# Giving out the tiles of the next moving operand up to two steps sooner in the feed-forward part of a layer, taking them at the split, and a rearranged last block

## The chip, the cores and the metric

One core of a Trainium2 chip runs the whole program. The metric is device time in microseconds (us), of one launch; lower is better. Engines are named as the profile names them: PE (TensorE matmuls), PEld (its weight loads), DVE (VectorE), ACT (ScalarE), POOL (GpSimd), SP (SyncE, which issues most of the transfers). L123 is a line of the kernel before. In the changed kernel the same statements stand 1 line further down after L1136, 10 further from the middle of `phases` on and up to 12 further in the last function.

## The reference

The kernel computes one layer of a streaming encoder on 2048 tokens of width 1024, in fp32: token mixing (sliding-window attention beside a gated recurrence), cross-attention into 256 memory tokens, and a SwiGLU feed-forward part of width 2816. Only the last part and the passage into it matter here:

```python
u = rms_norm(h, g_x_pre[l])
m = rms_norm(mem, g_mem[l])
y = cross_attention(u, m, wq_x[l], wk_x[l], wv_x[l], wo_x[l])
h = h + rms_norm(y, g_x_post[l])
u = rms_norm(h, g_ffn_pre[l])
y = (jax.nn.silu(u @ w_gate[l]) * (u @ w_up[l])) @ w_down[l]
h = h + rms_norm(y, g_ffn_post[l])
```

## The kernel before, in words

**Products.** A matrix product of fp32 accuracy is made of three matmuls of a reduced type: each operand is split into a high part (a rounded copy) and a low part (what the copy lacks), and `products` (L1270, L1271, L1272) issues high·high, high stationary·low moving, low stationary·high moving, for each of `nk` slices of 128 along the contraction. On top of that a block of 256 by 1024 outputs is made by seven products in place of eight (`seven`, a scheme of Strassen's kind). In the order of `STEPS` they are 1, 5, 6, 3, 7, 2, 4; each is `3·nk` matmuls of 128x512. Products 1, 6, 7 and 4 share one PSUM bank, 5 and 3 a second, 2 has a third, so a bank has to be emptied between them: products 1, 5 and 6 by a copy to a `part` tile (L1285 on ACT; L1287 on DVE where the last two blocks add something), the others by the block's own `out`.

**Jobs and blocks.** `phases` runs a list of jobs: 0 to 2 (attention output, scores, values; 8 blocks each), 3 and 4 (the feed-forward part's first product, one job per half of the tokens, 22 blocks each, gate and up in turn), 5, 6 and 7 (the down projection in three pieces of the contraction, nk = 3, 4, 4, 8 blocks of two row tiles each). Within a job the seven moving tiles `T` (one per product) stay in place over all blocks; the stationary tiles `S` are made anew for each block (`streamed`; ACT copies, DVE subtracts).

**Moving tiles.** There are seven slots for `T`, four in the pool `big` and three in `tb`. `uses` holds for each moving tile the steps that use it; a step `g` is one product. After each step, `half(g, ...)` looks whether the slot that comes free first is free by now (`free[1] > g`); if so it takes the next tile of the queue, allocates it, and starts the loads of its first half (the first slices of the contraction) into one or two `row` tiles (a pool of 12); at the next call its second half. It puts the half's split into `pending`, due at step `g + lag(k)`, where `lag` is 2 for tiles that are loaded ready-made. `split(g)` runs one due entry: it copies the half into the high part on ACT (L1106) and subtracts on DVE into the low part (L1109). In the last block of a job and the first of the next, a second `split(g)` a step, and after three of the steps a second `half`, are run. If a tile is needed whose halves aren't split, `Ready.__getitem__` forces them.

**What sets the order.** Each engine executes its instructions in one fixed order, which the tile scheduler derives from the program: it follows the written order as a priority and lets ready instructions pass others. `behind()` pins the splits behind the last ACT and DVE instructions written before them.

**Around the passage into job 3.** The value blocks of job 2 end with a chain (`value_block.after`): normalise (L1765), add (L1769), squares on ACT, factor on POOL, L1778 on DVE, transposes on PE and copies on ACT (L1532), stores to `u_d`, from which the moving tiles of jobs 3 and 4 are loaded. The hidden blocks evacuate with L1807 (DVE add), L1809 (Silu on ACT, with a table load when ACT's function set changes), L1816 and L1818.

**The last block.** `down_block.out` adds (L1856 or L1858), squares on ACT (L1641), multiplies by the gain in place (L1865, which must wait for the square's reading), then p_v and p_r on POOL (L1868, L1871), the final multiply-add on DVE (L1874) and a store by SP.

Of the kernel before, what the change touches and what calls it, by code (L numbers as in the profile page):

```python
# [12 lines left out]
F32R = mybir.dt.float32r  # L13
I32 = mybir.dt.int32
AF = mybir.ActivationFunctionType
ALU = mybir.AluOpType
AX = mybir.AxisListType

P = 128
T = 2048  # L20
# [10 lines left out]
EPS = 1e-6  # L31
# [17 lines left out]
class Layer:  # L49
# [1063 lines left out]
    def resident(self, get, nk, key, dst, keep, sums):  # L1113

        nc = self.nc
        halves = [(0, (nk + 1) // 2), ((nk + 1) // 2, nk)]

        def fetched(a, b):  # L1120
            if key in self.BLOCK:
                return get(*self.BLOCK[key], a, b - a), None
            if sums:
                return get(key, None, a, b - a), None
            if key == 5:
                return get(0, 1, a, b - a), get(0, 0, a, b - a)
            if key == 7:
                return get(1, 1, a, b - a), get(0, 1, a, b - a)
            if key == 6:
                return keep[7][len(src)], get(0, 0, a, b - a)  # L1130
            return get(1, 0, a, b - a), keep[6][len(src)]

        def split(a, b, t, o):
            if o is not None:
                nc.vector.tensor_tensor(t, t, o, ALU.add if key == 6 else ALU.subtract)
            self.split2(t, dst[:, 0, a:b], dst[:, 1, a:b], "A")  # L1136

        src = []
        for a, b in halves:
            t, o = fetched(a, b)  # L1140
            src.append(t)
            if key in (6, 7):
                keep[key] = src
            yield lambda a=a, b=b, t=t, o=o: split(a, b, t, o)
# [213 lines left out]
    def phases(self, jobs, first, prologue=None):  # L1358
# [13 lines left out]
        queue = sorted(uses, key=lambda k: (uses[k][0] - (5 if k[1] == 7 and jobs[k[0]][3] is None else 0), k))  # L1372
# [3 lines left out]
        T, keep = {}, [{} for _ in jobs]  # L1376
        current, left = [None], {}
        pending = []
# [19 lines left out]
        def lag(k):  # L1398
            return 2 if k[1] in self.BLOCK or jobs[k[0]][3] is not None else 0

        def split(g):

            if pending and pending[0][0] <= g:
                _, k, f = pending.pop(0)
                f()
                left[k] -= 1
                return True
            return False

        def half(g, tile):  # L1410

            if current[0] is None:
                if not queue:
                    return False
                free = min(slots, key=lambda s: s[1])
                if free[1] > g:
                    return False
                n, p, _ = k = queue.pop(0)
                slots.remove(free)
                slots.append((free[0], uses[k][-1], free[2]))  # L1420
                self._n += 1
                dst = (self.big if free[0] == "A" else self.tb).tile(
                    [P, 2, 4, 512], F32R, tag="big" if free[0] == "A" else "T", name=f"T_{self._n}",
                    bufs=4 if free[0] == "A" else 3)[:, :, :jobs[n][1]]
                T[k] = dst
                left[k] = 2
                current[:] = [(k, self.resident(fetch(n, tile), jobs[n][1], p, dst, keep[n], jobs[n][3] is not None)), 0]
            k, f = current[0]
            pending.append((g + lag(k), k, next(f)))
            current[1] += 1  # L1430
            if current[1] == 2:
                next(f, None)
                current[0] = None
            return True
# [43 lines left out]
        g = 0  # L1478
# [3 lines left out]
        for _, nk, bl, _, beside in jobs:  # L1482
            for i, (kind, _, out, follow, addend) in enumerate(bl):
                stream(at + 1)
                after += [f() for f in beside.get(i, ())]
                run = (self.seven(ready, Ready(), nk, out, addend) if kind == "s" else
                       self.eight(ready, Ready(), nk, out) if kind == "p" else
                       self.plain(ready, Ready(), nk, out, addend, kind))
                change = kind == "s" and i == len(bl) - 1
                for q in range(len(self.STEPS[kind])):  # L1490
                    for _ in range(1 if g or not first else 3):
                        next(run)
                        if first and g < 3:
                            yield
                    self.mark()
                    upto(need[g + 2])
                    if first and g == 1:
                        yield
                    for _ in range(1 if kind == "s" else 2):
                        for f in list(after):  # L1500
                            if next(f, after) is after:
                                after.remove(f)
                        if pending and lag(pending[0][1]):
                            with self.behind():
                                split(g)
                        else:
                            split(g)
                        if not first or g > 1:
                            half(g, self.row_tile)
                    if change or kind == "s" and fresh:  # L1510
                        split(g)
                        if change and q in (0, 3, 6):
                            half(g, self.row_tile)
                    g += 1
                after.append(follow())
                fresh = change
                at += 1
# [310 lines left out]
    def down_block(self, c, f0, nk, n):  # L1828
# [1 line left out]
        last = f0 + 2 * nk == NFF  # L1830
        end = last and n == NT - 2
        late = last and n >= NT - 4
        y, x, ss = {}, {}, []

        def stream(kind):
            if late:
# [11 lines left out]
        def out(i, j, a, b):  # L1848
# [12 lines left out]
            if end:  # L1861
                if not ss:
                    ss.append(self.small("q_s", 4))
                self.mean_square(d, ss[0][:, 2 * i + j:2 * i + j + 1])
                nc.vector.tensor_tensor(d, d, self.g_post[:, j * 512:(j + 1) * 512], ALU.mult)  # L1865
                if (i, 1 - j) in seen:
                    v = self.small("p_v")
                    nc.gpsimd.tensor_scalar(v, ss[0][:, 2 * i:2 * i + 1], ss[0][:, 2 * i + 1:2 * i + 2], EPS,  # L1868
                                            ALU.add, ALU.add)
                    r = self.small("p_r")  # L1870
                    nc.gpsimd.tensor_tensor(r, v, self.mhalf[:, 0:1], ALU.pow)  # L1871
                    for q in range(2):
                        sl = slice(q * 512, (q + 1) * 512)
                        nc.vector.scalar_tensor_tensor(y[i][:, sl], y[i][:, sl], r, x[i][:, sl], ALU.mult, ALU.add)  # L1874
                        self.store(self.out[(n + i) * P:(n + i + 1) * P, sl], y[i][:, sl])
                seen.append((i, j))

        seen = []
# [56 lines left out]
```

## Time and profile before

| what | value |
|---|---|
| median of 3 runs | 2514.67 us (2514.59 to 5079.82) |
| the profiled execution | 2514.36 us |
| its span, first to last instruction | 2512.7 us |
| mean granted TensorE clock | 0.998 |
| busy: PE, DVE, ACT, POOL | 99%, 72%, 50%, 13% |
| the program from job 3 on | from about 1235 us to the end |
| last matmul's start | 2503.63 us |

Rows of groups give line, engine, operation, output tile <- input tiles, form, count, then busy time and mean ns of one, then the idle time ahead and what ended it. Rows of the timeline give start and duration in us, and in brackets the idle time of that engine just before and what released it. Rows of windows give the stretch, its length, the busy time and count of the engine asked for, the granted clock, the busy share of the transfer engines and GB/s. A row of waits gives who waited for what: us in total, times, longest.

### The profile page before, as it was taken

The page shows a single profiled execution, that of the slowest core. Times are in us where ns is not written, and L with a number is a line of the kernel's source. Part 1 is how long each engine was busy: PE and PEld are TensorE (multiplying, and loading weights), DVE is VectorE, ACT ScalarE, POOL GpSimd, SP SyncE. Part 2 cuts the span into 40 slices and gives each one's busy share as a digit, 9 for nine tenths or more (in the row PEclk, how much of TensorE's full clock was granted, in tenths as well). Part 3 has the DMA queues.
Part 4 walks back from the last instruction along what each step waited for, and adds up shares of the span by engine and source line. Part 5 has one row for each costly group of instructions (what it writes and reads, how often), then busy time and mean ns, then how long its engine had stood idle before and what let it go on. Part 6 is the DMA issues. An engine that isn't in the chain of part 4 may idle for free.

```text
span 2512.7 us, 33669 instructions
## 1 busy us (share of the span) xinstructions
PE 2478.4 (99%) x11734; PEld 2064.5 (82%) x11734; DVE 1807.2 (72%) x2969; ACT 1245.6 (50%) x2554; POOL 318.4 (13%) x436
## 2 busy tenths in 40 slices
PE   9999999999999999999999999999999999999998
PEld 7777888888987878878878888888888888888886
DVE  8897588986658899988866655576666657564766
ACT  5464366755565575666743333353333344443543
POOL 5131232111301111101200000000000000000122
PEclk9999999999999999999999999999999999999999
DMA  7556865684988886858934422254454344565876
GB/s 218 164 180 168 239 208 173 207 264 153 332 314 281 292 296 194 268 185 263 350 114 168 143 76 84 92 184 160 144 192 171 114 147 141 190 164 117 229 168 156
DMA packets 360907, 483.81 MB, mean 193 GB/s; under 512 B 81056, under 2 KB 248992, under 8 KB 360736
## 3 DMA queue, kind: packets, MB, share of 16 engines
q1 hardware_dynamic: 352384, 451.24, 55.1%
q0 software_dynamic: 6048, 22.02, 5.2%
q10 hardware_dynamic: 2304, 8.39, 0.8%
q8 instruction: 92, 1.51, 0.2%
q14 instruction: 79, 0.65, 0.1%
HBM read 305.41 MB, written 176.16 MB: 192 GB/s over the span
## 4 chain that ended last, share of the span: by engine, by line
PE 85%; DVE 5%; DMA 4%; ACT 2%; issue 2%; POOL 1%; SPq 1%; DVEq 0%; ACTq 0%; POOLq 0%
PE psm L1272 22%; PE psm L1270 22%; PE psm L1271 22%; PE psg L156 3%; PE psg L157 3%; PE psg L158 3%; DVE S L1109 1%; DVE T L1109 1%; DMA row<-in_w_down_dram 1%; SPq L75 1%; PE pss L968 1%; DMA y_d<-yh 1%; PE pst L968 1%; ACT junk L1641 1%; PE pss L1531 0%
## 5 line engine op out<-in xcount | busy, mean ns | idle before, releaser
L1270 PE MATMUL psm<-T,S 128*128 128x512 f32 x2680 | 1035.1, 391 | 12.2 <-ACT part L1285 5.5
L1271 PE MATMUL psm<-T,S 128*128 128x512 f32 x2680 | 1043.2, 390 | 1.1 <-DVE T L1109 1.1
L1272 PE MATMUL psm<-T,S 128*128 128x512 f32 x2680 | 1030.8, 390 | 3.8 <-DVE S L1109 3.7
L1270 PEld LDWEIGHTS psm<-T,S 128*128 128x128 f32 x2680 | 503.2, 188 | 126.4 <-ACT part L1285 10.2
L1272 PEld LDWEIGHTS psm<-T,S 128*128 128x128 f32 x2680 | 503.4, 188 | 111.9 <-DVE S L1109 7.2
L1271 PEld LDWEIGHTS psm<-T,S 128*128 128x128 f32 x2680 | 503.5, 188 | 107.1 <-DVE T L1109 2.9
L1106 ACT ACTIVATE S<-sum 128x512 fp32r<-128x512 f32 (+1 forms) x370 | 223.1, 617 | 377.1 <-PE psm L1272 265.9
L1109 DVE TENSOR_TENSOR S<-sraw,S 128x512 fp32r<-128x512 f32 (+1 forms) x315 | 212.6, 680 | 229.1 <-ACT S L1106 227.1
L1285 ACT ACTIVATE part<-psm 128x512 f32<-128x512 f32 x285 | 168.6, 597 | 260.2 <-PE psm L1272 244.6
L1109 DVE TENSOR_TENSOR S<-sum,S 128x512 fp32r<-128x512 f32 (+1 forms) x388 | 258.4, 674 | 41.9 <-ACT S L1106 39.7
L1106 ACT ACTIVATE S<-sraw 128x512 fp32r<-128x512 f32 (+1 forms) x300 | 184.3, 617 | 111.6 <-PE psm L1272 109.7
L1109 DVE TENSOR_TENSOR T<-row,T 128x1024 fp32r<-128x1024 f32 (+1 forms) x112 | 130.9, 1184 | 29.0 <-ACT T L1106 27.0
L1674 POOL DMA_DIRECT2D y_d<-row x16 | 14.1, 879 | 1078.8 <-DVE row L1856 1027.8
L156 PE MATMUL psg<-u,whi 128*128 128x512 f32 x320 | 128.8, 402 | 0.1
L157 PE MATMUL psg<-u,whi 128*128 128x512 f32 x320 | 127.5, 398 | 0.0
L158 PE MATMUL psg<-u,wlo 128*128 128x512 f32 x320 | 126.8, 397 | 0.0
L1641 ACT ACTIVATE junk<-row 128x512 f32<-128x512 f32 x160 | 99.6, 623 | 47.1 <-DVE row L1663 18.7
L1106 ACT ACTIVATE T<-row 128x1024 fp32r<-128x1024 f32 (+1 forms) x112 | 112.9, 1027 | 11.6 <-DMA row<-d_s 5.0
L1807 DVE TENSOR_TENSOR row<-psm,part 128x512 f32<-128x512 f32 x66 | 44.1, 688 | 71.3 <-PE psm L1272 71.3
L1856 DVE TENSOR_TENSOR row<-psm,part 128x512 f32<-128x512 f32 x72 | 49.1, 688 | 47.8 <-PE psm L1272 47.7
L1816 DVE TENSOR_TENSOR part<-psm,part 128x512 f32<-128x512 f32 x66 | 43.8, 688 | 52.3 <-PE psm L1272 52.1
L1245 DVE TENSOR_TENSOR sum<-sraw,sraw 128x512 f32<-128x512 f32 (+1 forms) x97 | 65.2, 672 | 10.1 <-DMA sraw<-in_w_in_dram 4.9
(354 smaller groups left out, 3432.4 us busy)
## 6 DMA issues: line engine op xcount, KB each, us to landing
sraw<-in_w_gate_dram SPq DMA_DIRECT2D x44, 512.0 KB, 3.7
sraw<-in_w_up_dram SPq DMA_DIRECT2D x44, 512.0 KB, 3.5
hid_d<-row SPq DMA_DIRECT2D x44, 512.0 KB, 2.6
sraw<-hid_d SPq DMA_DIRECT2D x32, 512.0 KB, 4.3
sraw<-in_w_in_dram SPq DMA_DIRECT2D x48, 256.0 KB, 3.8
raw<-in_w_in_dram SPq DMA_DIRECT2D x20, 512.0 KB, 5.0
row<-in_w_down_dram SPq DMA_DIRECT2D x20, 512.0 KB, 7.3
row<-d_s SPq DMA_DIRECT2D x20, 512.0 KB, 8.1
```

The lines of the kernel that those rows point to most:

```text
L156: nc.tensor.matmul(ps, ah, bh, start=(i == 0), stop=False)
L157: nc.tensor.matmul(ps, ah, bl, start=False, stop=False)
L158: nc.tensor.matmul(ps, al, bh, start=False, stop=(i == n - 1))
L968: nc.tensor.transpose(ps[:, i * P:(i + 1) * P], S[2 * g + i // 2][:, i % 2, o + kb * P:o + (kb + 1) * P], self.ident)
L1106: self.nc.scalar.activation(hi, raw, AF.Copy)
L1109: self.nc.vector.tensor_tensor(lo, raw, f32(hi), ALU.subtract)
L1245: nc.vector.tensor_tensor(t, a, b, op)
L1270: nc.tensor.matmul(ps, s[:, 0, k, :], t[:, 0, k, :], start=st, stop=False, **kw)
L1271: nc.tensor.matmul(ps, s[:, 0, k, :], t[:, 1, k, :], start=False, stop=False, **kw)
L1272: nc.tensor.matmul(ps, s[:, 1, k, :], t[:, 0, k, :], start=False, stop=sp, **kw)
L1285: nc.scalar.activation(t, ps, AF.Copy)
L1641: self.nc.scalar.activation(junk, a, AF.Square, scale=float(D) ** -0.5, accum_out=to)
```

## The change

For jobs 3 to 7, `soon(k)` is 2: a slot counts as free up to two steps before its last use, so loads may start that much sooner, and the split is put down as due two steps later than before (`g + lag + soon`). The tile itself is no longer allocated when the slot is given out but at the first split of a half (`dst()`). In the last block of the program, product 2 is queued behind the last PE instruction written before it. In the last block's `out` the product with the gain goes to a new tile `yg`, p_v moves from POOL to DVE, and every second store of the output is issued by ACT's queue in place of SP's.

```diff
-            self.split2(t, dst[:, 0, a:b], dst[:, 1, a:b], "A")
+            d = dst()
+            self.split2(t, d[:, 0, a:b], d[:, 1, a:b], "A")
...
+        def soon(k):
+            return 2 if not first and k[0] >= 3 else 0
+
...
-                if free[1] > g:
+                if free[1] > g + soon(queue[0]):
                     return False
...
-                self._n += 1
-                dst = (self.big if free[0] == "A" else self.tb).tile(
-                    [P, 2, 4, 512], F32R, tag="big" if free[0] == "A" else "T", name=f"T_{self._n}",
-                    bufs=4 if free[0] == "A" else 3)[:, :, :jobs[n][1]]
-                T[k] = dst
+
+                def dst():
+                    if k not in T:
+                        self._n += 1
+                        T[k] = (self.big if free[0] == "A" else self.tb).tile(
+                            [P, 2, 4, 512], F32R, tag="big" if free[0] == "A" else "T", name=f"T_{self._n}",
+                            bufs=4 if free[0] == "A" else 3)[:, :, :jobs[n][1]]
+                    return T[k]
+
...
-            pending.append((g + lag(k), k, next(f)))
+            pending.append((g + lag(k) + soon(k), k, next(f)))
...
+                    behind = [self.traced(mybir.EngineType.PE)] if at == len(blocks) - 1 and not first and q == 5 else []
                     for _ in range(1 if g or not first else 3):
-                        next(run)
+                        with self.queued(*behind):
+                            next(run)
...
-                nc.vector.tensor_tensor(d, d, self.g_post[:, j * 512:(j + 1) * 512], ALU.mult)
+                if i not in yg:
+                    yg[i] = self.row_tile()
+                nc.vector.tensor_tensor(yg[i][:, j * 512:(j + 1) * 512], d, self.g_post[:, j * 512:(j + 1) * 512], ALU.mult)
...
-                    nc.gpsimd.tensor_scalar(v, ss[0][:, 2 * i:2 * i + 1], ss[0][:, 2 * i + 1:2 * i + 2], EPS,
+                    nc.vector.tensor_scalar(v, ss[0][:, 2 * i:2 * i + 1], ss[0][:, 2 * i + 1:2 * i + 2], EPS,
                                             ALU.add, ALU.add)
...
-                        nc.vector.scalar_tensor_tensor(y[i][:, sl], y[i][:, sl], r, x[i][:, sl], ALU.mult, ALU.add)
-                        self.store(self.out[(n + i) * P:(n + i + 1) * P, sl], y[i][:, sl])
+                        nc.vector.scalar_tensor_tensor(yg[i][:, sl], yg[i][:, sl], r, x[i][:, sl], ALU.mult, ALU.add)
+                        (nc.scalar.dma_start if q else self.store)(self.out[(n + i) * P:(n + i + 1) * P, sl], yg[i][:, sl])
```

How this moves instructions shows at three places. The first is ACT at the first block of job 3. Before, `psm_2024` is the bank of products 1, 6, 7 and 4, `psm_2036` that of 5 and 3; the three `part` rows empty the bank after products 1, 5 and 6; T_1997 is the moving tile of product 3, T_2007 of product 7, T_2019 of product 2:

```order
L1106 ACTIVATE T_1997_12659<-row_1998_12660 128x1024
L1106 ACTIVATE T_1997_12659<-row_2001_12677 128x1024
L1285 ACTIVATE part_2025_12793<-psm_2024_12780 128x512
L1106 ACTIVATE T_2007_12714<-row_2008_12715 128x1024
L1106 ACTIVATE S_2049_12907<-sraw_1978_12559 128x512
L1285 ACTIVATE part_2037_12832<-psm_2036_12819 128x512
L1106 ACTIVATE T_2007_12714<-row_2011_12723 128x1024
L1106 ACTIVATE S_2051_12929<-sraw_1978_12559 128x512
L1532 ACTIVATE row_1949_12441<-pss_2040_12839 128x512
L1532 ACTIVATE row_1949_12441<-pss_2041_12845 128x512
L1285 ACTIVATE part_2043_12868<-psm_2024_12780 128x512
L1106 ACTIVATE T_2019_12768<-row_2020_12769 128x1024
```

Now, with `psm_2020` the bank of products 1, 6, 7 and 4, T_2044 is the tile of product 3, T_2047 of product 7 and T_2052 of product 2:

```order
L1286 ACTIVATE part_2039_12856<-psm_2020_12768 128x512
L1106 ACTIVATE T_2044_12878<-row_1995_12653 128x1024
L1106 ACTIVATE T_2052_12930<-row_2017_12762 128x1024
L1106 ACTIVATE S_2054_12950<-sraw_2018_12764 128x512
L1106 ACTIVATE S_2059_12977<-sum_2058_12975 128x512
L1819 ACT_TABLE_LOAD
L1819 ACTIVATE row_2045_12895<-row_2045_12895 128x512
L1106 ACTIVATE T_2047_12903<-row_2005_12708 128x1024
```

The first half of product 3's tile was copied ahead of the evacuation of product 1 and is now behind that of product 6, the product just ahead of it; product 7's first half was copied ahead of the evacuation of product 5 and is now behind the first Silu, which follows product 3.

The second place is ACT at the first block of job 4, where PE is given the first matmul of product 2 alone, ahead of the next block's product 1. Before, T_2515 is product 2's tile and row_2516 its first half:

```order
L1106 ACTIVATE T_2506_15915<-row_2507_15916 128x1024
L1285 ACTIVATE part_2522_15987<-psm_2511_15924 128x512
L1106 ACTIVATE T_2515_15946<-row_2516_15947 128x1024
L1106 ACTIVATE S_2533_16056<-sraw_2509_15920 128x512
L1106 ACTIVATE S_2535_16076<-sum_2534_16074 128x512
L1809 ACTIVATE row_2527_16011<-row_2527_16011 128x512
```

Now T_2528 is product 2's tile and row_2507 its first half:

```order
L1286 ACTIVATE part_2523_15988<-psm_2511_15924 128x512
L1106 ACTIVATE T_2521_15971<-row_2504_15893 128x1024
L1106 ACTIVATE S_2533_16056<-sraw_2509_15920 128x512
L1106 ACTIVATE S_2535_16076<-sum_2534_16074 128x512
L1106 ACTIVATE S_2541_16100<-sum_2540_16098 128x512
L1819 ACTIVATE row_2526_16009<-row_2526_16009 128x512
L1106 ACTIVATE T_2528_16015<-row_2507_15916 128x1024
```

The copy of product 2's first half went from ahead of the first Silu to behind it.

The third place is PE in the last block. Before, product 4 (T_3389) follows product 7 (T_3370) in the same bank:

```order
L1270 MATMUL psm_3576_22233<-T_3370_21146,S_3594_22306 128x512
L1271 MATMUL psm_3576_22233<-T_3370_21146,S_3594_22306 128x512
L1272 MATMUL psm_3576_22233<-T_3370_21146,S_3594_22306 128x512
L1270 MATMUL psm_3576_22233<-T_3389_21229,S_3601_22351 128x512
L1271 MATMUL psm_3576_22233<-T_3389_21229,S_3601_22351 128x512
L1272 MATMUL psm_3576_22233<-T_3389_21229,S_3601_22351 128x512
```

Now product 2 (T_3392), in a bank of its own, follows product 7 (T_3385):

```order
L1271 MATMUL psm_3576_22233<-T_3385_21204,S_3594_22306 128x512
L1272 MATMUL psm_3576_22233<-T_3385_21204,S_3594_22306 128x512
L1273 MATMUL psm_3576_22233<-T_3385_21204,S_3594_22306 128x512
L1271 MATMUL psm_3604_22356<-T_3392_21247,S_3600_22333 128x512
L1272 MATMUL psm_3604_22356<-T_3392_21247,S_3600_22333 128x512
L1273 MATMUL psm_3604_22356<-T_3392_21247,S_3600_22333 128x512
```

Product 2's twelve matmuls stood ahead of product 3's and stand now between those of products 7 and 4.

More of the change, by code (lines that the diff above doesn't have):

```diff
@@ L1832, in down_block @@
         late = last and n >= NT - 4
-        y, x, ss = {}, {}, []
+        y, x, ss, yg = {}, {}, [], {}
         def stream(kind):
```

## The prediction

> All line numbers are those of the kernel before. A "product" is one of the seven of a block, in the order 1, 5, 6, 3, 7, 2, 4; "T of product 3" is that product's moving tile, made from two loaded halves: ACT copies a half into the high part (L1106), DVE subtracts to get the low part (L1109).
>
> **What bounds the kernel now.** I read the page's busy shares first.
>
> ```profile
> span 2512.7 us, 33669 instructions
> PE 2478.4 (99%) x11734; PEld 2064.5 (82%) x11734; DVE 1807.2 (72%) x2969; ACT 1245.6 (50%) x2554; POOL 318.4 (13%) x436
> L1106 ACT ACTIVATE T<-row 128x1024 fp32r<-128x1024 f32 (+1 forms) x112 | 112.9, 1027 | 11.6 <-DMA row<-d_s 5.0
> ```
>
> PE is busy 99% of the span, so the change can win only what PE still waits. The change touches the program from the passage into job 3 (the first feed-forward job) on, so I next took PE's waits from 1235 us to the end:
>
> ```profile
> PE psm L1270 <- DVE row L1856: 2.3, 2, 1.4
> PE psm L1271 <- DVE T L1109: 1.1, 2, 0.8
> PE psm L1270 <- ACT part L1285: 0.7, 1, 0.7
> PE psm L1270 <- ACT T L1106: 0.2, 1, 0.2
> PE psm L1270 <- DVE part L1287: 0.2, 1, 0.2
> ```
>
> That is 4.5 us in all, of which only 1.3 are waits for a T. Then the places, by windows of PE at the passages into jobs 3, 4, 5 and 6, in the last block but one and in the last, and the pace of a stretch without waits:
>
> ```profile
> 1250.00:1264.00 14.00, 12.79 (x51) 1.00 0.68 236
> 1660.00:1680.00 20.00, 19.31 (x85) 1.00 0.44 149
> 2070.00:2090.00 20.00, 20.00 (x90) 1.00 0.48 157
> 2190.00:2212.00 22.00, 20.24 (x87) 1.00 0.98 346
> 2465.00:2475.00 10.00, 9.84 (x43) 1.00 0.84 166
> 2494.00:2504.00 10.00, 9.12 (x40) 1.00 0.63 105
> 1700.01 0.39 PE L1272 MATMUL psm<-T,S 128*128 128x512 f32 x1
> 1702.73 0.39 PE L1270 MATMUL psm<-T,S 128*128 128x512 f32 x1
> ```
>
> Between the last two rows lie twelve starts, 2.72/12 = 0.227 us each; a product of twelve takes 2.72. By that pace the windows lose 14 − 51×0.227 = 2.4, then 0.7, nothing, 2.3, 0.2 and 0.9: 6.5 us. Nothing that this change can remove is larger, 0.3% of the time, while a comparison of this kernel tells about 2% from no change.
>
> **The change, part by part.** *1. The split is due two steps later (jobs 3 to 7).* At the passage into job 3 the loads stand at about the same places of SP's order as before, so they don't come sooner; but the splits stand one or two products later on ACT and DVE. These are the rows of before that I price it with:
>
> ```profile
> 1234.11 1.28 DVE L1778 SCALAR_TENSOR_TENSOR row<-row,q_r,extra 128x1024 f32<-128x1024 f32 x1 [1.66 <-DMA out_dram<-row]
> 1235.31 2.35 DVE L1109 TENSOR_TENSOR T<-row,T 128x1024 fp32r<-128x1024 f32 x2
> 1237.59 0.68 DVE L1109 TENSOR_TENSOR S<-sum,S 128x512 fp32r<-128x512 f32 x1
> 1238.19 1.28 DVE L1778 SCALAR_TENSOR_TENSOR row<-row,q_r,extra 128x1024 f32<-128x1024 f32 x1
> 1241.72 2.47 DVE L1765 SCALAR_TENSOR_TENSOR row<-row,q_r,g 128x1024 f32<-128x1024 f32 x2
> 1239.06 0.60 ACT L1285 ACTIVATE part<-psm 128x512 f32<-128x512 f32 x1
> 1254.08 1.28 ACT L1809 ACT_TABLE_LOAD   x1 [2.13 <-DVE row L1807]
> 1255.38 0.64 ACT L1809 ACTIVATE row<-row 128x512 f32<-128x512 f32 x1
> 1255.91 1.04 ACT L1106 ACTIVATE T<-row 128x1024 fp32r<-128x1024 f32 x1
> 1258.27 0.50 PE L1271 MATMUL psm<-T,S 128*128 128x512 f32 x1 [0.35 <-DVE T L1109]
> 1262.06 1.22 POOL L1656 TENSOR_TENSOR q_r<-q_w,mhalf 128x2 f32<-128x2 f32 x1
> 1276.76 0.39 PE L1270 MATMUL psm<-T,S 128*128 128x512 f32 x1
> 1234.20:1256.00 21.80, 21.80 (x25) 1.00 1.03 371
> ```
>
> On DVE a following row starts 1.20 after an L1778 or L1765, 1.14 after a T and 0.60 after an S; on ACT 0.95 after a T, 0.5 after the rest, 1.28 after the table load. I walked the changed orders of PE, ACT, DVE and POOL forward from 1234.1 with these, each instruction starting when its engine is free and its inputs are there. The last row is a window of DVE: 21.80 us busy of 21.80, so a row put later there is done later. The walk gives these waits of PE in block 1 of job 3:
> - Product 6: its first half is subtracted behind ten other DVE rows (four of 1.20, two of 1.14, four of 0.60, 9.5 us), waits 0.4 for POOL's factor among them and ends at 1245.3, where PE arrives at 1242.9: 2.4. Its second half stands four rows further (two T, two S, with its own 1.22): 2.7.
> - Product 3: the ACT copy of its first half stands behind the evacuation of product 6, which PE must first finish: 0.49 + 1.06, then DVE's 1.2 with what little PE can do meanwhile: 2.9.
> - Product 7: its first half stands on ACT behind the table load and the first Silu, which wait for product 3's evacuation on DVE: 0.68 + 1.28 + 0.52 + 1.06 and the hops, 3.9 at the first matmul, then 1.0 for DVE's subtraction at the second: 4.9.
> - Four pairs of transposes behind product 7 wait for L1778, whose factor comes off ACT's squares and POOL's power (1.22) with two small steps ahead of it, which have slid along: 2.7.
> - Product 2: its first half stands behind the second Silu, after L1807: 1.7.
>
> Sum 17.3 in place of 2.4: **+14.9**. Product 1 of block 2, at 1276.76 before, comes at about 1292. Bounds: not below −2.4 (all of today's waits gone); if each wait shows half of the walk, +6; if no two of these chains overlap (product 3 and 7 each the full 3.6 + 1.2 and the transposes' whole chain again), about +20. I take the walk, since every row in it has a duration from the trace.
>
> At the passage into job 4 the same happens once. PE is given a lone first matmul of product 2 ahead of the next block's product 1, and ACT copies its half behind a Silu that waits for L1807.
>
> ```profile
> 1673.97 0.68 DVE L1807 TENSOR_TENSOR row<-psm,part 128x512 f32<-128x512 f32 x1
> 1674.69 0.63 ACT L1809 ACTIVATE row<-row 128x512 f32<-128x512 f32 x1 [1.63 <-DVE row L1807]
> 1675.22 1.04 ACT L1106 ACTIVATE T<-row 128x1024 fp32r<-128x1024 f32 x1
> ```
>
> Today the same lone matmul has its half copied before that Silu. Behind later DVE rows L1807 starts at about 1675.7, so the copy ends 0.68 + 0.52 + 1.06 and hops later, 1678.1, and PE has been ready since 1675.8: 2.3, and 0.6 in product 7 before it, 2.9 in place of 0.7: **+2.2** (bounds −0.7, +3.5).
>
> *2. The slot given out up to two steps sooner.* Into jobs 5, 6 and 7 the loads do move forward. The largest wait there is
>
> ```profile
> 2198.58 0.50 PE L1270 MATMUL psm<-T,S 128*128 128x512 f32 x1 [1.45 <-DVE row L1856]
> ```
>
> DVE's L1856 was late behind a T split that waited for its load; this goes (−1.6), but splits for products 1 and 6 come later by 0.65, 1.1 and 1.3 by the same walk. I take +0.4, +0.5 and +0.5 for the three passages, **+1.4** (bounds −2.5, +4). What a tile taken at the split costs or saves by itself is nothing: no instruction is added.
>
> *3. The last block.*
>
> ```profile
> 2500.22 0.69 DVE L1856 TENSOR_TENSOR row<-psm,part 128x512 f32<-128x512 f32 x1 [0.49 <-PE psm L1272]
> 2501.06 0.47 PE L1270 MATMUL psm<-T,S 128*128 128x512 f32 x1 [0.88 <-DVE row L1856]
> 2506.79 0.79 POOL L1868 TENSOR_SCALAR p_v<-q_s 128x1 f32<-128x1 f32 x1 [2.91 <-ACT junk L1641]
> 2507.67 0.57 POOL L1871 TENSOR_TENSOR p_r<-p_v,mhalf 128x1 f32<-128x1 f32 x1
> 2508.27 1.41 DVE L1874 SCALAR_TENSOR_TENSOR row<-row,p_r,row 128x512 f32<-128x512 f32 x2 [0.86 <-POOL p_r L1871]
> ```
>
> Product 4 waits 0.9 to 1.1 until DVE has emptied product 7's bank; with product 2's twelve matmuls (2.72) now between, the wait is covered, −1.1. But product 2's evacuation, square and pow then come after it, and DVE's final pair for the first row tile stands ahead of product 4's evacuation. p_v on DVE instead of POOL: bounds 0.1 and 0.8, and I take 0.15, the small end, since the operation handles one column. The walk ends DVE's last pair at 2508.05 in place of 2508.27 + 1.41 = 2509.68: **−1.6**. Issuing the last store from ACT changes who issues, not the transfer; 0 (±0.5).
>
> Sum: 14.9 + 2.2 + 1.4 − 1.6 = +16.9, on the profiled execution's own 2514.36 (span 2512.7 and 1.7 around it): **2531.3**. That execution lies 0.3 under the median of 2514.67.
>
> **Rivals.** *Only the last block counts.* If ACT and DVE at the passages are in truth ahead of the walk, the waits keep their size: 2514.4 − 1.6 = 2512.8. For it: today's order also has T splits behind a Silu and loses only 2.4 there. Against it: DVE is without a gap from 1234 to 1256, so nothing can be ahead.
>
> *Sooner loads pay (faster than before).* If the earlier slots let every half be loaded and split in time, the 6.5 us of PE's losses go, and the tail gives 0.5 more: 2514.4 − 7.0 = 2507.4. It decides where waits end on a DMA; the page shows 5.0 us of such waits on ACT (row<-d_s), but PE's own wait list holds 1.3 us for a T. Against it: into job 3 the loads aren't sooner.
>
> *The clock drops in the new gaps.* After PE's last matmul, which starts at 2503.6, the windows (us, PE busy, granted clock) go on so:
>
> ```profile
> 2507.00:2508.00 1.00, 0.00 (x0) 0.86 0.00 0
> 2508.00:2509.00 1.00, 0.00 (x0) 0.50 0.00 0
> ```
>
> The clock halves at 2507.7, some 3.7 us after PE stopped. The walk has one gap of 3.9 and several of 2.3 to 2.9. If four of them each bring as long at half clock as the drop took, 3.7 us in which half the work is done, that is 4 × 1.85 = 7: 2538. Against it: around today's gaps, 1.45 at most, the windows stay at 1.00. The Trainium skill, "TensorE: Matmul & The Clock Gate", Part 1, has the array at half clock after an idle window of about 3.4 us and at full clock after a busy one; the windows after the end agree with it, and by that rule one or two gaps could cost, 2533 to 2535.
>
> **Chances.** The walk 0.66; last block only 0.15; sooner loads 0.12; the clock on top of the walk 0.07. The likeliest one's own range, from the bounds of its largest term, is 2522 to 2537. To hold 8 in 10 I take 2511 to 2538, which leaves out the faster rival and the extremes. No case reaches 2% (50 us): faster 0.01, same 0.98, slower 0.01.
>
> **What would show it.** Right: PE's waits from 1235 on sum to some 20 us, most of them on T (ACT L1106, DVE L1109) and on L1778 before transposes, between 1242 and 1272; block 2's product 1 at about 1292; the lone matmul of product 2 near 1690 waits over 2 us; no wait of product 4 in the last block. Wrong: the windows at the passage into job 3 show PE losing under 6 us, or DVE with gaps there that end on DMAs.

## The result and the profile after

The changed kernel takes 2543.74 us in the median of four runs (2541.38 to 2546.35) against 2514.63 before: ratio 1.0115, 95% interval 1.0103 to 1.0127. It is slower, by 29 us or 1.2%, clear of the noise though under the 2% below which the prediction calls two times the same; the forecast was 17 more and the range ended at 2538. One of before's four runs took 5079.82 us, a slow one, which the ratio leaves out. The profiled execution took 2541.38 with a span of 2539.7, 27.0 more than before's.

The waits of PE from 1235 us to the end, in the changed kernel (who waited for whom; us in total, times, longest). Line numbers are now those of the changed kernel: L1271, L1272, L1273 are the three matmuls, L1286 the copy to a part.

```profile
PE psm L1271 <- ACT T L1106: 9.2, 5, 3.7
PE psm L1272 <- DVE T L1109: 5.7, 6, 1.9
PE psm L1271 <- ACT part L1286: 5.0, 1, 5.0
PE pss L1541 <- ACT row L1542: 0.3, 1, 0.3
```

4.5 us of waits have become 20.2, and those for a T have gone from 1.3 to 14.9; the wait of product 4 in the last block is gone. That is most of what the prediction asked for. Two things differ: no wait of the transposes for L1778 (now L1788) is in the list, and 5.0 us are spent on one wait for a part, which the prediction did not have. Product 1 of block 2 came at 1295.5 in place of 1292.

But 20.2 − 4.5 is 15.7, not 27. To place the rest I compared the starts of the matmuls in the two traces. Both have 11734 in nearly the same order, so the difference between the n-th starts is the delay so far; read at seven places in stretches without waits (before's 1233, 1425, 1880, 2152, 2290 and 2427 us, and the last matmul), its steps give each passage its own price. What follows the last matmul is the tail.

| kernel | up to job 3 | into 3 | into 4 | into 5 | into 6 | into 7 | last blocks | tail | span |
|---|---|---|---|---|---|---|---|---|---|
| forecast | 0 | +14.9 | +2.2 | +0.4 | +0.5 | +0.5 | −1.6 with the tail | | +16.9 |
| changed kernel | +1.1 | +17.6 | +4.1 | +0.8 | −1.0 | +6.8 | −1.6 | −0.8 | +27.0 |
| last_only | +7.3 | +0.1 | 0.0 | 0.0 | +0.1 | +0.9 | −1.6 | −0.8 | +6.0 |
| late_only | −0.9 | +16.4 | +11.1 | +3.1 | +1.3 | +9.1 | −1.6 | −0.1 | +38.4 |
| soon_j57 | +2.3 | +0.3 | 0.0 | +0.8 | −0.8 | +6.1 | −1.6 | −0.8 | +6.1 |
| pool_loads | −1.8 | +0.3 | 0.0 | +0.8 | −0.4 | −0.1 | −1.6 | −0.4 | −3.4 |
| fill | 0.0 | +15.4 | +4.1 | +0.8 | −0.6 | +6.7 | −1.6 | −0.8 | +23.9 |
| soon1 | −0.4 | +14.9 | −0.6 | +0.3 | +0.6 | +0.1 | +0.1 | −0.8 | +14.1 |
| on_time | +0.2 | −0.2 | −0.6 | 0.0 | −0.9 | −0.2 | −1.6 | −0.8 | −4.2 |
| asap | +3.1 | +0.8 | −0.6 | 0.0 | −2.8 | +0.1 | −1.6 | −0.8 | −1.8 |
| mix | +2.1 | 0.0 | −0.6 | 0.0 | −2.8 | +0.1 | −1.6 | −0.8 | −3.6 |
| on_time4 | −0.5 | +0.1 | −0.8 | 0.0 | −0.9 | −0.2 | −1.6 | −0.8 | −4.7 |
| tail_only | +0.4 | −0.1 | 0.0 | 0.0 | −0.9 | 0.0 | −0.5 | −1.3 | −2.5 |
| queue_only | +0.8 | −0.1 | 0.0 | 0.0 | −1.2 | +1.2 | −1.6 | +0.5 | −0.4 |

The first column is the same program in all of them: it differs by −1.8 to +7.3 from one execution to the next. So a whole time tells little below 3 us here, while a passage with nothing changed repeats within 0.3 into jobs 3 to 5. Into jobs 6 and 7 it does so only within about 1.2 (last_only, tail_only and queue_only have the same give-out as before there).

Two things make up what the waits don't. First, PE ran at half clock after some of its gaps. Windows of PE in the changed kernel (us, length, busy, count, granted clock, transfer share, GB/s), into job 3 and then into jobs 4 and 7:

```profile
1245.00:1250.00 5.00, 2.82 (x9) 0.93 1.00 326
1250.00:1255.00 5.00, 2.69 (x6) 0.50 1.03 330
1255.00:1260.00 5.00, 4.64 (x11) 0.55 0.97 343
1260.00:1265.00 5.00, 1.17 (x2) 0.79 0.45 144
1265.00:1270.00 5.00, 4.86 (x13) 0.52 0.00 0
1270.00:1275.00 5.00, 3.41 (x20) 1.00 0.09 27
1696.00:1700.00 4.00, 3.82 (x10) 0.57 0.38 131
2385.00:2390.00 5.00, 4.27 (x12) 0.66 0.27 101
```

The starts show what that costs; PE at the lone matmul of product 2 in job 4 and after:

```profile
1696.18 1.02 PE L1271 MATMUL psm<-T,S 128*128 128x512 f32 x2 [2.24 <-ACT T L1106]
1696.99 0.63 PE L1272 MATMUL psm<-T,S 128*128 128x512 f32 x1
1697.42 0.63 PE L1273 MATMUL psm<-T,S 128*128 128x512 f32 x1
...
1699.92 0.39 PE L1273 MATMUL psm<-T,S 128*128 128x512 f32 x1
```

Starts 0.43 apart in place of 0.227 for 3.4 us after a gap of 2.24: 1.9 us. Adding up what starts between 0.3 and 0.44 us apart take beyond 0.227 gives 4.7, 1.9 and 1.7 us into jobs 3, 4 and 7; before, 1.1, 0.2 and 0.1, all of it single starts behind short waits and none at half clock. The difference is 6.9 of the 27. A busy PE in the profile hides this: its busy time rose by 10 us.

Second, the passage into job 7. ACT, then PE there in the changed kernel, then SP's transfers, now and before:

```profile
2384.13 1.06 ACT L1106 ACTIVATE T<-row 128x1024 fp32r<-128x1024 f32 x1 [6.54 <-DMA row<-in_w_down_dram]
2385.09 0.58 ACT L1286 ACTIVATE part<-psm 128x512 f32<-128x512 f32 x1
```

```profile
2385.73 0.64 PE L1271 MATMUL psm<-T,S 128*128 128x512 f32 x1 [5.02 <-ACT part L1286]
```

```profile
2361.18 0.37 SPq L75 DMA_DIRECT2D sraw<-hid_d  x1
2361.64 1.23 SPq L75 DMA_DIRECT2D row<-in_w_down_dram  x2
2368.90 0.37 SPq L75 DMA_DIRECT2D sraw<-hid_d  x1
2369.37 0.92 SPq L75 DMA_DIRECT2D row<-d_s  x2
2370.38 0.90 SPq L75 DMA_DIRECT2D row<-in_w_down_dram  x2
2371.33 1.24 SPq L75 DMA_DIRECT2D row<-d_s  x2
```

```profile
2339.47 0.37 SPq L75 DMA_DIRECT2D sraw<-hid_d  x1
2339.94 1.99 SPq L75 DMA_DIRECT2D row<-d_s  x2
2342.02 0.90 SPq L75 DMA_DIRECT2D row<-in_w_down_dram  x2
2342.98 1.16 SPq L75 DMA_DIRECT2D row<-d_s  x2
2344.24 1.31 SPq L75 DMA_DIRECT2D row<-in_w_down_dram  x2
2346.33 0.34 SPq L75 DMA_DIRECT2D row<-d_s  x1
2348.06 0.37 SPq L75 DMA_DIRECT2D sraw<-hid_d  x1
2356.25 0.33 SPq L75 DMA_DIRECT2D row<-d_s  x1
```

PE waited for a part, the part's copy for ACT, and ACT stood in a T split whose half had not landed. That half is the second of the two `row<-in_w_down_dram` at 2370.38; it was issued at 2370.82 and landed at 2384.11, 13.3 us later. Job 7 has fourteen halves. Six of them are issued in one burst, because they stand on SP behind the second of two loads of stationary operands, `sraw<-hid_d`, that had to wait for its buffer. Before, only one half stood behind that load. Counted from the same matmuls, the fifth to the eighth half and the last are issued 2.8 to 12.3 us sooner than before, but the ninth to the thirteenth 2.3 to 3.7 us later. The half that ACT stood for is the twelfth: it was issued 3.2 us later and landed 2.8 us later than before.

### The profile page after: what moved, and what is told of

It is laid out like the page before. It is cut to its first block, busy times and chain, and to the rows that moved or that the text cites. A ratio compares the mean times of both kernels' runs of the same rounds, so it can differ in the third digit from the quotient of the medians.

```text
span 2539.7 us, 33669 instructions
## 1 busy us (share of the span) xinstructions
PE 2488.5 (98%) x11734; PEld 2071.9 (82%) x11734; DVE 1807.0 (71%) x2971; ACT 1246.1 (49%) x2554; POOL 310.8 (12%) x434
## 4 chain that ended last, share of the span: by engine, by line
PE 79%; DVE 7%; DMA 5%; ACT 3%; issue 3%; SPq 1%; POOL 1%; DVEq 0%; ACTq 0%; POOLq 0%
PE psm L1273 21%; PE psm L1272 21%; PE psm L1271 21%; PE psg L156 3%; PE psg L158 3%; PE psg L157 3%; DVE T L1109 1%; DVE S L1109 1%; DMA y_d<-yh 1%; ACT junk L1651 1%; DVE sum L1246 1%; ACT T L1106 1%; SPq L75 1%; PE pss L968 1%; DMA row<-in_w_down_dram 1%
## 5 line engine op out<-in xcount | busy, mean ns | idle before, releaser
L1271 PE MATMUL psm<-T,S 128*128 128x512 f32 x2680 | 1037.7, 392 | 24.4 <-ACT part L1286 10.6
L1272 PE MATMUL psm<-T,S 128*128 128x512 f32 x2680 | 1047.7, 392 | 5.9 <-DVE T L1109 5.7
L1273 PE MATMUL psm<-T,S 128*128 128x512 f32 x2680 | 1035.4, 391 | 3.8 <-DVE S L1109 3.8
L1271 PEld LDWEIGHTS psm<-T,S 128*128 128x128 f32 x2680 | 505.0, 189 | 138.1 <-ACT part L1286 14.4
L1272 PEld LDWEIGHTS psm<-T,S 128*128 128x128 f32 x2680 | 505.5, 189 | 114.3 <-DVE T L1109 10.0
L1273 PEld LDWEIGHTS psm<-T,S 128*128 128x128 f32 x2680 | 505.7, 189 | 111.7 <-DVE S L1109 7.0
L1286 ACT ACTIVATE part<-psm 128x512 f32<-128x512 f32 x285 | 168.3, 596 | 279.8 <-PE psm L1273 263.8
L1684 POOL DMA_DIRECT2D y_d<-row x16 | 14.1, 878 | 1095.0 <-DVE row L1866 1046.7
L1651 ACT ACTIVATE junk<-row 128x512 f32<-128x512 f32 x160 | 99.6, 624 | 34.7 <-DVE row L1673 20.2
L1246 DVE TENSOR_TENSOR sum<-sraw,sraw 128x512 f32<-128x512 f32 (+1 forms) x97 | 66.0, 680 | 13.3 <-DMA vb_d<-pair 5.6
```

Source lines behind the costliest of these rows:

```text
L1246: nc.vector.tensor_tensor(t, a, b, op)
L1271: nc.tensor.matmul(ps, s[:, 0, k, :], t[:, 0, k, :], start=st, stop=False, **kw)
L1272: nc.tensor.matmul(ps, s[:, 0, k, :], t[:, 1, k, :], start=False, stop=False, **kw)
L1273: nc.tensor.matmul(ps, s[:, 1, k, :], t[:, 0, k, :], start=False, stop=sp, **kw)
L1286: nc.scalar.activation(t, ps, AF.Copy)
L1651: self.nc.scalar.activation(junk, a, AF.Square, scale=float(D) ** -0.5, accum_out=to)
```

## The experiments

**last_only.** `soon` returns 0 for every job; the rest of the change stays.

```diff
-            return 2 if not first and k[0] >= 3 else 0
+            return 0
```

> The change with soon set to 0 for every job: tiles taken at the split and the last block's edits stay, give-out and due step are those of before. Theory (the whole loss comes from the splits being due two steps later and from what the sooner give-out does to the load queue, the last block's edits gain): the passages lose as before and the end comes 2 to 2.5 us sooner than before, about 2512.3. Rival (taking the tile at the split costs something by itself, or the last block gains nothing): 2514.6 or more.

Measured: 2513.98 in the median against 2514.43, ratio 1.0001 (0.9992 to 1.0010). By the table, −2.4 from the last blocks on, as the theory had it, and no passage lost more than 0.9; the whole time, between the theory's 2512.3 and the rival's 2514.6, does not show it; the part up to job 3 took 7.3 longer in the profiled execution. `soon` makes the loss; the last block's edits gain.

**late_only.** The old test for a free slot, with the splits still two steps later.

```diff
-                if free[1] > g + soon(queue[0]):
+                if free[1] > g:
```

> The change with the old test for a free slot, so nothing is given out sooner, but every split of jobs 3 to 7 is still due two steps later. Theory (late splits make the loss): the passage into job 3 loses the same 17 to 18 us as in the change, the one into job 4 at least its 4, the last block gains 2.4, in all 2536 to 2548. Rival (the sooner give-out makes the loss): about 2512.

Measured: 2555.07, ratio 1.0163 (1.0146 to 1.0180); 16.4 into job 3, 11.1 into job 4, 3.1, 1.3 and 9.1 after. The rival falls: with nothing given out sooner the loss is larger, 11 us more than in the change. The later splits alone make the loss into jobs 3 and 4; the sooner give-out takes part of it back from job 4 on. The whole is 7 above the 2536 to 2548 that was expected, because the passages from job 4 on lose more than was thought. Into job 7 the loss is 9.1 though nothing is given out sooner: in this trace eight of the fourteen halves are issued behind the second stationary load.

**soon_j57.** `soon` is 2 for jobs 5, 6 and 7 only (`k[0] >= 5`).

> The change with soon kept at 2 for jobs 5, 6 and 7 alone, 0 for jobs 3 and 4. Theory: the losses at the passages into jobs 3 and 4 (17.6 and 4.1 more than before) go, those into jobs 5 to 7 stay (+0.8, -1.0, +6.8), the last block gains 2.4: 2514.6 + 6.6 - 2.4 = 2518.8. Rival (the wait at job 7 comes from how the earlier passages shifted the phase): about 2512.

Measured: 2520.48, ratio 1.0024 (1.0015 to 1.0033). Jobs 3 and 4 as before, +0.8, −0.8 and +6.1 after, within 0.7 of what was expected. The losses into jobs 5 to 7 do not need those into jobs 3 and 4.

**pool_loads.** The kernel of soon_j57 with the loads of job 7's tiles issued by POOL.

```diff
+                own = self.load
+                if not first and n == 7:
+                    self.load = self.nc.gpsimd.dma_start
                 if j is None:
...
+                self.load = own
```

> The kernel of soon_j57, with the loads of job 7's moving tiles issued by POOL's queue in place of SP's. Theory (the 6.1 us lost at the passage into job 7 come from six loads that stand on SP behind a stationary load that waits for its buffer): the passage loses 0 to 2. Rival (the transfer engines are simply full there): 4 or more stay lost.

Measured in one execution: −0.1 into job 7, in place of +6.1. The same halves, as large and in the same program, are there in time once they don't stand behind the stationary load: counted from the same matmuls, the twelfth is issued 4.0 us sooner than in soon_j57 and lands 6.4 us sooner. So it was not that the transfer engines had no room for these bytes; the place in the queue was the limit.

**fill.** The changed kernel with PE kept at work in its gaps.

```diff
-    def seven(self, S, T, nk, out, addend):
+    def seven(self, S, T, nk, out, addend, fill=False):
...
+            if fill and p in (6, 3, 7):
+                t1 = T[1]
+                extra = self.bank("s")
+                with self.queued(done):
+                    for _ in range(9):
+                        nc.tensor.matmul(extra, t1[:, 0, 0, 0:P], t1[:, 0, 0, :], start=True, stop=True,
+                                         skip_group_check=True)
             self.products(ps, [(s, t, nk)], p in (1, 5, 2), p in (4, 3, 2))
+            if fill:
+                done = self.traced(mybir.EngineType.PE)
...
-                run = (self.seven(ready, Ready(), nk, out, addend) if kind == "s" else
+                run = (self.seven(ready, Ready(), nk, out, addend, not first and at == 24) if kind == "s" else
```

> The change, and in the first block of job 3 nine extra matmuls into an unused bank ahead of each of products 6, 3 and 7 (27 x 0.227 = 6.1 us of PE work that nothing reads), so that PE works while it waits there. Theory (the matmuls 0.43 apart behind each wait are PE at half clock because it stood idle): the granted clock stays at 1.00 between 1245 and 1275, no starts 0.43 apart, and the passage into job 3 loses 12 to 15 us against before in place of 17.6, although PE has 6.1 us more to do. Rival (something else slows these matmuls, such as DVE and ACT at the same memory): they stay 0.43 apart, and the passage loses 17 or more.

Measured in one execution: PE's windows into job 3 now read

```profile
1250.00:1255.00 5.00, 2.83 (x13) 1.00 1.05 287
1255.00:1260.00 5.00, 3.74 (x17) 1.00 0.96 345
1260.00:1265.00 5.00, 3.29 (x12) 1.00 0.35 120
1265.00:1270.00 5.00, 3.13 (x8) 0.70 0.00 0
```

The clock stays at 1.00 up to 1265, where it was 0.50 to 0.79, and the starts 0.43 apart fall from 21 to 7: they remain only behind one gap of 2.55 us (as late starts) that nine matmuls did not fill. The passage loses 15.4 in place of 17.6 although 27 matmuls were added, and into job 4, where nothing was filled, the clock drops as before. That gap kept the loss a little above what was expected (12 to 15) and some slow starts where none were expected; where the gaps were filled the theory holds, and the rival (slow starts all the same, 17 or more) falls. The transposes behind product 7 also moved later in PE's order here, so the 2.2 are not the clock's alone.

**soon1.** One step in place of two.

```diff
-            return 2 if not first and k[0] >= 3 else 0
+            return 1 if not first and k[0] >= 3 else 0
```

> The change with soon 1 in place of 2, so slots given out one step sooner and splits due one step later. Theory (each step of lateness takes 2.7 us of cover; six loads of job 7 now stand ahead of the second stationary load): the passage into job 3 loses between 4 and 11 us more than before, into job 7 0 to 1, with the last block 2516 to 2526. Rival (any lateness breaks the cover, so the loss is that of two steps): 2530 or more.

Measured: 2529.61, ratio 1.0059 (1.0045 to 1.0073). Job 7 came as expected (+0.1), and its loads stand ahead of the second stationary load. Into job 3 the theory (4 to 11) was wrong and the rival nearly right: 14.9, close to that of two steps. ACT there:

```profile
1253.81 1.06 ACT L1106 ACTIVATE T<-row 128x1024 fp32r<-128x1024 f32 x1 [4.81 <-DMA row<-u_s]
1254.89 1.28 ACT L1819 ACT_TABLE_LOAD   x1
1256.18 0.63 ACT L1819 ACTIVATE row<-row 128x512 f32<-128x512 f32 x1
1256.72 1.04 ACT L1106 ACTIVATE T<-row 128x1024 fp32r<-128x1024 f32 x1
```

Product 7's second half stood behind the table load and the Silu, and these behind another T split whose half had not landed: 4.81 us, and PE waited 5.1 for product 7. The granted clock was at half from 1250.9 to 1271.4 there. So the loss does not grow by a fixed amount per step. It depends on which instruction a split lands behind, and on whether the split ahead of it has its data.

**on_time.** Slots given out sooner as in the change, but a split due two steps after its load or after its slot is free, whichever is later.

```diff
+        came = {}
...
+                came[k] = free[1]
                 slots.append((free[0], uses[k][-1], free[2]))
...
-            pending.append((g + lag(k) + soon(k), k, next(f)))
+            pending.append((max(g, came[k]) + lag(k), k, next(f)))
```

> The change with the sooner give-out, but each split due at two steps after its slot is free or its load is issued, whichever is later, so that no split is due later than before. Theory (late splits make the loss at jobs 3 and 4, and rows held longer push six loads behind a stationary load at job 7): the passage into job 3 loses what it did before, into job 4 0 to 3 more or less, no wait of 5 us at job 7; with the last block 2508 to 2514. Rival (sooner loads by themselves crowd the queue): the 5 us wait at job 7 stays, 2518 or more.

Measured: 2509.52, ratio 0.9979 (0.9970 to 0.9988), 0.2% faster than before and faster than the change. ACT's order into job 3 is that of before again, and so is the passage's price. The last eight loads of job 7 stand ahead of the second stationary load, in SP's rows:

```profile
2339.45 0.37 SPq L75 DMA_DIRECT2D sraw<-hid_d  x1
2339.92 0.97 SPq L75 DMA_DIRECT2D row<-in_w_down_dram  x2
2340.94 1.13 SPq L75 DMA_DIRECT2D row<-d_s  x2
2342.13 1.47 SPq L75 DMA_DIRECT2D row<-in_w_down_dram  x2
2343.69 1.18 SPq L75 DMA_DIRECT2D row<-d_s  x2
2348.88 12.52 SPq L75 DMA_DIRECT2D sraw<-hid_d  x2
```

No wait is left at job 7, so the rival, that sooner loads by themselves crowd the queue, falls. Together with late_only this shows what put the loads behind the stationary one: the later due step, with or without the sooner give-out. That it does so through the row tiles, which are held until the split, was expected, but no run tests it alone. Of the 4.2 us that the span lost, 2.4 are the last blocks' and 0.6 those into job 4; the 0.9 into job 6 is within what that passage varies.

**asap and mix.** In asap splits are due at their old lag behind the load, or when the slot is free; mix does so for job 6 only, and is on_time otherwise (`came` as in on_time).

```diff
-            pending.append((max(g, came[k]) + lag(k), k, next(f)))
+            pending.append((max(g + lag(k), came[k]), k, next(f)))
```

```diff
-            pending.append((max(g, came[k]) + lag(k), k, next(f)))
+            pending.append((max(g + lag(k), came[k] + (0 if k[0] == 6 else lag(k))), k, next(f)))
```

> The change with each split due at its old lag behind the load or when its slot is free, whichever is later, so up to two steps sooner than in on_time. Theory (late splits cost, sooner ones give cover): the passages into jobs 4 to 7 lose no more than in on_time (1.8 less than before in all), total 2506 to 2511. Rival (a split put sooner waits for its load and holds up ACT and DVE, in-order): the passages lose 2 or more, 2512 or more.

> The kernel of on_time, but the tiles of job 6 split as soon as their slot is free, as in asap, and the others as before. Theory (asap's gain of 2.8 at the passage into job 6 and on_time's elsewhere add up): job 3 0, job 4 -0.6, job 5 0, job 6 -2.8, job 7 -0.2, the last blocks -2.4 against before, -6.0 in all: 2508 to 2509. Rival (they don't add up, the splits of job 6 put sooner hold up something later): 2510 or more.

Measured: asap 2510.91, ratio 0.9984 (0.9975 to 0.9994); mix 2509.88, ratio 0.9982 (0.9973 to 0.9991). asap lies in the range that was expected and its rival falls, though it loses 0.8 into job 3. Both gain 2.8 into job 6, about all that before lost there (up to 1.2 of it is within what that passage varies), and mix has the passages that were expected of it: 0.0, −0.6, 0.0, −2.8, +0.1 and the last blocks −2.4, −5.7 in all. Its whole time lies between the 2508 to 2509 of the theory and the 2510 of the rival and cannot be told from on_time's; the part up to job 3 was 2.1 longer in the profiled execution. In PE's waits of mix from 1235 us on, of 4.5 us are left

```profile
PE psm L1272 <- DVE T L1109: 1.1, 2, 0.8
PE psm L1271 <- ACT part L1286: 0.2, 1, 0.2
```

**on_time4.** on_time with four steps in place of two in `soon`.

> The kernel of on_time with slots given out up to four steps sooner. Theory (the twelve row tiles and the place behind the stationary loads limit what sooner loads can do): nothing gained over on_time, the passages into jobs 4 to 7 lose 0 to 2 more than in it. Rival (more lead is more cover): 1 or more less.

Measured in one execution: every passage within 0.4 of on_time. More lead gives nothing.

**queue_only and tail_only.** last_only without the edits of `down_block.out`, and last_only without the pin of product 2 (`behind = []`).

> Soon 0 for every job and the end of the last block as before, with only the pin that keeps product 2 behind product 7 (and the tile taken at the split). Theory: from the last block's start to PE's last matmul 1.15 less than before, as in last_only; from there to the end of the span more than in last_only, since product 2's evacuation now comes late into a chain with POOL's 0.8 us p_v and the in-place product: 0 to +2 against before. Rival (the gain in PE needs the new row tile too): less than 0.5 gained in PE.

> Soon 0 for every job, with the last block's new row tile, p_v on DVE and the stores from ACT, but without the pin of product 2. Theory: PE's wait in the last block stays (no gain there), the chain after PE's last matmul ends 0.4 to 1.5 sooner than before; the 0.47 gained ahead of the last block does not come from the pin and stays. Rival (that 0.47 is the pin's): it goes.

Measured in one execution each. queue_only: −1.6 until PE's last matmul and +0.5 after it; tail_only: −0.5 and −1.3. Both rivals fall. So the pin is worth 1.15 in PE and costs 0.5 in the old tail, and the new tail is worth 1.3 alone; both together, with the 0.47 that comes ahead of the last block, give 2.4. That 0.47 comes with neither of them: it is there in every kernel with the tile taken at the split but soon1, which loses 1.2 at the same place. Why, no run tells apart.

## Why the prediction was wrong, point by point

The direction held, and so did the mechanism at the first two passages. The measured time lies 5.7 us above the range, because one term of the sum was mis-sized, and because the clock, which the prediction gave a chance of 0.07 on top of its sum, did drop. Either alone would have stayed inside: 2543.7 less the 6.3 that the passage into job 7 took beyond its +0.5 is 2537.4, and less the clock's 6.9 it is 2536.8 (1.6 is in both).

**The step that failed: "Into jobs 5, 6 and 7 the loads do move forward", and with it "I take +0.4, +0.5 and +0.5 for the three passages".** Into job 7 it was +6.8, and the three together 6.6, beyond their bound of +4. The first eight halves of job 7 and the last do come as early or earlier, but five come later, behind a second stationary load on SP, and the split that waited 6.5 us for one of them stood on ACT ahead of the evacuation that PE needed. The prediction shows windows of the passages into jobs 3 to 6 and none of the one into job 7, and it did not work out what the later due step does to the place of loads on SP. soon_j57 and pool_loads show this cause: the loss is there without the other passages, and gone when the loads don't stand on SP. late_only (+9.1) and on_time (−0.2) show that the later due step puts them there and the sooner give-out does not.

**"The clock drops in the new gaps", 0.07, 2538.** It dropped four times, at three passages, and cost 6.9 us (8.3 of slow starts less before's 1.4). The price of 1.85 an event was right (1.9 and 1.7 at the two clear ones), and four events, 7.4 rounded to 7 in the prediction, come near the 6.9. That there were four is luck, since the condition was wrong. From the end of the trace the prediction has PE stand for 3.7 us before the clock halves; a gap of 2.24 was enough into job 4. A drop stood in before's own trace too, at 811.3 us, behind gaps of 0.78 and 0.85 us and outside the part that the prediction looked at. And a rival whose cause, the gaps, is the forecast's own mechanism belongs in the sum. The rule quoted from the Trainium skill, "TensorE: Matmul & The Clock Gate", Part 1, an idle window of about 3.4 us, gave one or two events; there were four, one of them after a single gap of 2.24 us and one after gaps of 1.34 and 1.90 us. Its time back to full clock agrees: 3.4 us of slow starts into job 4.

**Into job 3, +14.9.** Measured 17.6, of which 3.6 are slow starts beyond before's; without those it is 14.0. Its waits, counted as late starts, came as follows: product 6 1.5 and 2.5 (2.4 and 2.7), product 3 3.3 (2.9), product 7 5.2 (4.9), transposes 0.8 (2.7), product 2 1.4 (1.7). Only the transposes and product 6's first half are clearly off. PE reached the transposes late, at the half clock of product 7, which would leave little of their chain to wait for; no run tests that alone. late_only has 16.4 without any sooner give-out, so it is the split's lateness.

**Into job 4, +2.2.** Measured 4.1: the waits were 3.2 (2.9) in place of 0.8, and the other 1.7 is the clock.

**Into jobs 5 and 6, +0.9.** Measured −0.2. **The last block, −1.6.** Measured −2.4: the wait of 1.1 in PE went as said; p_v took 0.21 on DVE in place of POOL's 0.79 (0.15 taken); 0.47 came ahead of the block, with a cause left open.

**The other rivals.** "Only the last block counts" and "sooner loads pay" were wrong for the change, but the second is what on_time and mix do, by 1.9 and 3.3 at the passages, once the splits are no later: well short of the 6.5 us at stake, and partly within the 1.2 by which the passage into job 6 varies.

## What to carry to other kernels

A lead taken at one end of a chain must not be given back at the other: loads given out sooner pay only if the work behind them is not due later, and `max(g, free) + lag` says that where `g + lag + soon` does not. When loads or the splits behind them are moved, read what each load now stands behind in its queue and which engine will stand still for it in order, and price the instruction behind that one too. And where a forecast opens gaps of 2 us or more in PE, half-clock time after them (1.7 to 1.9 us for each clear drop here) belongs in the sum.

## What the runs showed of the hardware

The half clock set in after a gap of 2.24 us into job 4 of the changed kernel, while before's gaps of up to 1.45 from job 3 on left the windows at 1.00, and so did one of 2.17 in the kernel fill, nearly as long. So the length of a gap alone does not decide. The granted clock in the traces shows more: within each trace all its changes lie a whole number of 3.413 us apart, so the clock goes by a fixed grid of time, whatever the matmuls do. Windows of PE on that grid, two of the changed kernel's into job 4, then two of fill's into job 3 (the count in brackets takes in matmuls that began before the window):

```profile
1693.02:1696.43 3.41, 1.17 (x5) 1.00 0.26 101
1696.43:1699.84 3.41, 3.41 (x9) 0.50 0.45 154
1249.98:1253.38 3.40, 1.76 (x8) 1.00 0.95 283
1253.39:1256.79 3.40, 2.87 (x13) 1.00 1.06 279
```

The gap into job 4 lies whole in one window of the grid, where four matmuls start, and the next window is at half clock. The gap in fill is cut in two by an edge, six matmuls start in the window with the longer part, and the clock stays. At full pace fifteen starts fit. From 1230 us to the last matmuls, over the traces of all fourteen kernels, each of the thirteen windows at full clock with five starts or fewer was followed by half clock, and none with six or more. A drop lasted one window, 3.41 us, and more where further gaps followed (6.83 and 10.24 into job 3), with matmuls starting 0.43 apart; their own duration in these rows is 0.63 in place of 0.39. After PE's last matmul of before it took 3.7 us to show.
